# Packing the weight folds of a decoder kernel into earlier projection steps, and moving one memory head's transposes

## The chip, the cores and the metric

The kernel runs on one core of a Trainium2 chip. The metric is the device time of one execution in microseconds (us). A core has several engines that work at the same time, each through its own list of instructions in order: TensorE (PE in the rows of the profile: matmuls and transposes), VectorE (DVE), ScalarE (ACT: copies with scaling, and functions such as Exp, whose tables it must load first), GpSimd (POOL), and SyncE (SP), which issues nearly all DMAs of this kernel. An engine that reaches an instruction whose input is not there waits, and everything behind that instruction on the same engine waits with it.

## The reference, cut to what matters

One layer of a decoder for 2048 prompt tokens (and 32 sample tokens, which play no part here): a mixer, an attention to 256 memory tokens, and a gated MLP.

```
def mixer(xn, s0, lp):
    q, k, v, r, a, u, sv = split_cols(xn @ w_in)
    logg = jax.nn.log_sigmoid((a @ w_alpha + b_alpha)) / GLA_TAU
    o, S = gla_chunked(q, k, v, logg, s0)
    o = rmsnorm(o, g_gla_out).reshape(B, T, GLA_WIDTH) * jax.nn.silu(r)
    sv = rmsnorm(jax.nn.gelu(sv), g_sgu)
    s_out = jax.nn.gelu(u) * sgu_spatial(sv, w_s, b_s)
    return jnp.concatenate([o, s_out], -1) @ w_out, S, sv

def mem_kv(mem, g_mem, wk_x, wv_x):
    mn = rmsnorm(mem, g_mem)
    return mn @ wk_x, mn @ wv_x          # 256 x 4 heads x 256 each

def mem_attend(hn, mk, mv, wq_x, wo_x):
    q = hn @ wq_x
    p = softmax(q @ mk.T * MEM_DH ** -0.5)        # by head
    return (p @ mv) @ wo_x
```

## The kernel before, in words

**Numbers in two parts.** Each product of fp32 matrices is made of three matmuls on parts of lower precision (`mm3`, lines 100 to 102): high by high, high by low, low by high. So each weight that arrives is split: ACT copies it into a high part (`h_...`, line 85), DVE subtracts to get the low part (`l_...`, line 86). A weight tile of 128 x 1024 costs one such instruction on each of the two engines.

**Folding.** The scores of the memory attention are x wq mkT. The kernel multiplies wq by the memory keys once (`fold_qk`), and the memory values by wo once (`fold_vo`), writes both results to DRAM, and later streams them in as if they were weights. The keys and values of the four heads are made first (`mem_proj`, tiles mkp and mvp), turned by transposes for the output (mkt, mvt), and stored in DRAM (kd, vd) from which a fold loads them again (kr, vr; line 606). A fold of wq with keys is a pair of steps, for 4 heads x 2 halves: `turn_wq` loads a raw piece of wq (r_wqf) and transposes it (tile wqp; ACT and DVE split it into wqh and wql), and `fold_qk` makes 24 matmuls on two tiles qkp, which ACT copies (qkf) and splits (qkh). That gives 16 steps, `qk_steps`. A fold of wo with values is one step, again for 4 heads x 2 halves (`vo_steps`, 8 steps): a weight r_wof is split, 12 matmuls fill two tiles vop, which are split into voh and vol and put to DRAM.

**The order.** The prompt is worked on in four sub-blocks of 512 tokens. In the first one, the main steps are numbered 0 to 18: 0 to 3 the projection sv (four weights r_ws, tiles t_ws), 4 the projection a (tile ap), 5 k (weights r_wk, tiles a_wk), 6 q (r_wq, a_wq), 7 to 10 v (r_wv, t_wv), 11 and 12 u (a_wu), 13 to 16 r (t_wr), 17 and 18 the first half of the output projection (a_wo). A function `weave` puts side steps between them: `(steps, first, last)` spreads the steps evenly over main steps first to last. The side steps beside the folds are those of the gated linear attention: the gates of the decay (lgp on PE, then lgt on ACT: Abs, Exp, Ln for two halves, each Exp and each Ln behind a table load), the decayed keys and scores (e, kr, s, P), the state (ktp, kt, kv) and the outputs (op, o, otp), and the spatial gate (zp, z). Weights are loaded up to five units ahead of their step (`AHEAD`), into five raw buffers (`NRAW`) that come free when a weight is split. Within this written order a scheduler, at build time, sets the order of each engine's list; on the chip each engine follows its list strictly. The transposes `mkt` of a memory head stand in the steps of `mem_proj`, ahead of the first sub-block, where PE also turns the tokens themselves (xt, line 803).

The change touches `mem_proj` (line 577) and the line that sets the two spreads of the folds (line 1813). PSUM banks matter at two places: accumulators (`acc`: t_ws, a_wk, t_wv and so on) and the rest (`mps`: wqp, qkp, vop, lgp) have four banks each.

Of the kernel before, what the change touches and what calls it, by code (L numbers as in the profile page):

```python
# [38 lines left out]
def hymba_step_kernel(  # L39
# [22 lines left out]
    def U(name, dt=F32):  # L62
        return up.tile([128, TM], dt, tag="U", name=name)
# [7 lines left out]
    def acc(name):  # L71
        return accp.tile([128, 512], F32, tag="acc", name=name)

    def mps(name):
        return mmp.tile([128, 512], F32, tag="mm", name=name)
# [8 lines left out]
    def split(hi, lo, src, lo_eng=None):  # L84
        act.activation(hi, src, AF.Copy)  # L85
        (lo_eng or dve).tensor_tensor(lo, src, hi.bitcast(F32), ALU.subtract)  # L86
# [12 lines left out]
    def mm3(ps, wh, wl, xh, xl, first, last):  # L99
        out = pe.matmul(ps, wh, xh, start=first, stop=False)  # L100
        pe.matmul(ps, wh, xl, start=False, stop=False)  # L101
        pe.matmul(ps, wl, xh, start=False, stop=last)  # L102
        return out
# [23 lines left out]
    def wready(src, name):  # L127

        def load():
            out = []  # L130
            for x, tag in enumerate(("whi", "wlo")):
                t = wp.tile(list(src.shape[0:1]) + list(src.shape[2:]), F32R, tag=tag, name=f"{tag}_{name}")
                nc.sync.dma_start(t.bitcast(F32), src[:, x])
                out.append(t)
            return tuple(out)
        return load
# [220 lines left out]
    def keep(t, pattern, base, cm):  # L357
        pool.affine_select(out=t, in_=t, pattern=pattern, compare_op=ALU.is_ge, fill=0.0,
                           base=base, channel_multiplier=cm)
# [125 lines left out]
    def weave(main, *sides):  # L485

        out = []
        due = [0.0] * len(sides)
        at = [0] * len(sides)
        for i, m in enumerate(main):  # L490
            out.append(m)
            for j, (steps, first, last) in enumerate(sides):
                if i < first:
                    continue
                due[j] = len(steps) * min(1.0, (i - first + 1) / (last - first + 1))
                while at[j] < len(steps) and at[j] < due[j] - 1e-9:
                    out.append(steps[at[j]])
                    at[j] += 1
        for j, (steps, _, _) in enumerate(sides):
            out += steps[at[j]:]  # L500
        return out
# [33 lines left out]
    mem_st = NS_()  # L535
# [41 lines left out]
    def mem_proj(nm, h, od, *ws):  # L577

        th, tl, tf = U(f"m{nm}h{h}", F32R), U(f"m{nm}l{h}", F32R), U(f"m{nm}f{h}")
        for dt in range(2):  # L580
            ps = acc(f"m{nm}p{h}{dt}")
            ds_ = slice(dt * 128, (dt + 1) * 128)
            for k in range(8):
                wh, wl = ws[k // 4]
                mm3(ps[:, :256], wh[:, k % 4, ds_], wl[:, k % 4, ds_], *mem_st.pair[k], k == 0, k == 7)
            s = slice(dt * 256, (dt + 1) * 256)
            dve.tensor_tensor(tf[:, s], ps[:, :256], mem_st.bc[:, :256], ALU.mult)
            split(th[:, s], tl[:, s], tf[:, s])
        for x, t in enumerate((th, tl)):
            nc.sync.dma_start(kvd[nm, h][:, x], t[:, :512].bitcast(F32))  # L590
        if h % 2 == 0:
            mem_st.out[nm] = [U(f"m{nm}o{h}{c}") for c in range(2)]
        for c in range(2):
            ps = mps(f"m{nm}t{h}{c}")
            for d in range(2):
                pe.transpose(ps[:, d * 128:(d + 1) * 128], tf[:, d * 256 + c * 128:d * 256 + (c + 1) * 128], ident)
            dve.tensor_copy(mem_st.out[nm][c][:, (h % 2) * 256:(h % 2 + 1) * 256], ps[:, :256])
            if h % 2:
                nc.sync.dma_start(od[c * 128:(c + 1) * 128, (h - 1) * 256:(h + 1) * 256], mem_st.out[nm][c][:, :512])
# [60 lines left out]
    def fold_vo(h, jh, wu):  # L660

        if jh == 0:
            again("v", h)
        vh, vl = mem_st.t["v"]
        wh, wl = wu
        flush()
        for mt in range(2):
            ps = mps(f"vop{h}{jh}{mt}")
            for dt in range(2):
                a = dt * 256 + mt * 128  # L670
                mm3(ps, vh[:, a:a + 128], vl[:, a:a + 128], wh[:, dt], wl[:, dt], dt == 0, dt == 1)
            hi, lo = U(f"voh{h}{jh}{mt}", F32R), U(f"vol{h}{jh}{mt}", F32R)
            split(hi[:, :512], lo[:, :512], ps)
            kk = 2 * h + mt
            for x, t in enumerate((hi, lo)):
                put(vod[kk // 4][:, 2 * jh:2 * jh + 2, x, kk % 4],
                    t[:, :512].bitcast(F32).rearrange("p (m c) -> p m c", m=2))

    mem_steps = []
    for nm, w, od in (("k", wk_x, o_mem_k), ("v", wv_x, o_mem_v)):  # L680
        od = od[0, 0].rearrange("m h d -> m (h d)")
# [3 lines left out]
    qk_steps = []  # L685
    for h, j in ((2 * i + hh, j) for i in range(2) for j in range(2) for hh in range(2)):
        qk_steps.append(Step(lambda a, h=h, j=j: turn_wq(h, j, a), [wraw_unit(wq_x[0], 4 * j, 4, h * 256, 256, f"wqf{h}{j}")]))
        qk_steps.append(Step(lambda h=h, j=j: fold_qk(h, j)))
    vo_steps = [Step(lambda a, h=h, jh=jh: fold_vo(h, jh, a), [(wo_x[0], 2 * h, 2, jh * 512, 512, f"wof{h}{jh}")])
                for h in range(4) for jh in range(2)]  # L690
# [158 lines left out]
    def carry_sample(B, prev):  # L849

        def fn():
            for k in range(8):
                pool.tensor_tensor(B.h[k][:, SB:TM], prev.h[k][:, SB:TM], smp.d[:, k * NS:(k + 1) * NS], ALU.add)
        return Step(fn)
# [946 lines left out]
    for s, B in enumerate(blocks):  # L1801
        proj = proj_steps(B)
        gla, gtail = gla_steps(B)
        nlast = 4 if B.mix_sample else 3
        sgu_st = sgu_steps(B)
        nst = len(sgu_st) - 4
        keep = None
        if B.mix_sample:
            def keep():
                if not hasattr(smp, "x"):  # L1810
                    smp.x = U("smpx")
                return smp.x
        w1, w2, stat = out_proj_steps(B, lambda k0, m2, s=s: (w_out[0], k0, 4, m2 * 256, 256, f"wo{s}{k0}{m2}"),
                                      lambda B=B: B.cat, "gx", "wo", B.mix_sample, 4, B.mix_sample, keep, seven=True, whole=not B.mix_sample)
        early = [Step(sample_conv)] if B.ffn_sample else []
        folds = [(qk_steps, 0, 10), (vo_steps, 11, 19)] if s == 0 else []
        steps += weave(proj + w1, *folds, (after, 0, 5), (sgu_st[:1], 6, 6), (early, 1, 1), (sgu_st[1:nst], 11, 11), (sgu_st[nst:nst + 2], 12, 13), (sgu_st[nst + 2:], 16, 16), (gla[:1], 4, 4), (gla[1:2], 6, 6), (gla[2:12], 8, 10), (gla[12:-nlast], 10, 13), (gla[-nlast:], 16, 16), (gtail, 16 + B.mix_sample, 18 + B.mix_sample))
        scales, sc, turns = attention_steps(B)
        x1, x2, xstat = out_proj_steps(B, lambda k0, m2, s=s: wready(vod[k0 // 4][:, m2], f"wx{s}{k0}{m2}"),
                                       lambda B=B: B.ao, "gffn", "wx", False, 0, B.ffn_sample, seven=s > 0, whole=True)  # L1820
        steps += w2 + [stat, scales]
        steps += weave(sc + x1, (turns[:2], 8, 9), (turns[2:3], 13, 13), (turns[3:], 14, 14))
        fstart, fmain, flast = ffn_steps(B, s == NSB - 1)
        B.xstat = xstat.fn
        steps += x2 + ([xstat, fstart] if s == 0 else [])
        sides = []
        if B.mix_sample:
            sides.append((sample_steps(), 1, len(fmain) - 5))
        if s + 1 == NSB:
            ncs = conv_out_steps(carry, 2, o_state_conv[0, 0], "nc")  # L1830
            sides.append((ncs[:4], 30, 36))
        steps += weave(fmain[:-4], *sides)
        if s + 1 < NSB:
            after = final_steps(B)
            nxt = blocks[s + 1]
            norm = norm_in_steps(nxt)
            if nxt.ffn_sample:
                norm.append(carry_sample(nxt, B))
            steps += weave(fmain[-4:] + flast, (norm, 0, 4))
            if B.ffn_sample:  # L1840
                after += conv_out_steps(sct, 16, o_state_conv_s[0].rearrange("b t f -> (b t) f"), "ncs")
        else:
            steps += fmain[-4:-2] + flast[:1] + fmain[-2:] + ncs[4:] + flast[1:]
            after = []
# [30 lines left out]
```

## Time and profile before

| quantity | value |
|---|---|
| median of 3 runs | 2819.22 us (2818.85 to 2822.41) |
| the profiled execution's own time | 2823.05 us |
| its span (first to last instruction) | 2821.3 us |
| PE busy | 2784.2 us, 99% |
| DVE busy | 1902.5 us, 67% |
| ACT busy | 1108.3 us, 39% |
| POOL busy | 564.6 us, 20% |
| mean granted TensorE clock | 0.995 |

The stages that the change touches lie in the first 300 us: the memory heads and the tokens up to some 72 us, sv until 104, k and q until 140, v, u and r from there to 249, the output projection's first half from 271. Everything after that is the same program in both versions, except for what it inherits.

In rows of the trace the first number is the start in us from the beginning of the span, the second how long the instruction (or a run of like ones) took, then engine, line, operation, output and inputs with shapes; in square brackets the time that the engine had been idle before it, and what ended the wait.

### The profile page before, as it was taken

Reading aid. Unit: us, or ns where it says so; the run is one execution under the profiler, and the core shown is the slowest. Engines: PE = TensorE matmul, PEld = TensorE weight load, DVE = VectorE, ACT = ScalarE, POOL = GpSimd, SP = SyncE. Lnnn points to the kernel's source line nnn. Section 1 sums busy time; section 2 is a strip of 40 time slices with the busy share of each in tenths; the row PEclk is TensorE's granted clock in tenths of the full one; section 3 lists DMA queues with packets and bytes.
Section 4 is the critical chain, followed back from the end, with each engine's and each line's share of the span. In section 5 each row is a group of like instructions: output and inputs, shape, how many; then the busy total and the mean of one; then the engine's idle time right before and its main releaser. Section 6 shows DMA issues by size and latency. Waiting matters only on the chain.

```text
span 2821.3 us, 46765 instructions
## 1 busy us (share of the span) xinstructions
PE 2784.2 (99%) x17756; PEld 2459.7 (87%) x17756; DVE 1902.5 (67%) x3285; ACT 1108.3 (39%) x1948; POOL 564.6 (20%) x636
## 2 busy tenths in 40 slices
PE   8999999999999999999999999999999999999998
PEld 8787888888877898998888889899999788899997
DVE  6677778777657786655545778666666688665555
ACT  5645545333353444322223445422223645431222
POOL 1002212111101231322311121232221013132222
PEclk9999999999999999999999999999999999999999
DMA  9755589999942246888886325567776323577775
GB/s 296 245 193 195 174 262 332 341 340 348 351 129 62 83 145 214 305 292 291 318 315 214 93 66 193 209 243 258 255 266 227 109 75 137 202 261 274 271 281 181
DMA packets 369546, 638.06 MB, mean 226 GB/s; under 512 B 27356, under 2 KB 238272, under 8 KB 369322
## 3 DMA queue, kind: packets, MB, share of 16 engines
q1 hardware_dynamic: 369322, 635.07, 66.0%
q8 instruction: 141, 2.31, 0.3%
q14 instruction: 83, 0.68, 0.1%
HBM read 507.56 MB, written 127.41 MB: 225 GB/s over the span
## 4 chain that ended last, share of the span: by engine, by line
PE 90%; DVE 4%; DMA 2%; ACT 2%; issue 1%; POOL 1%; DVEq 0%; SPq 0%; ACTq 0%; POOLq 0%
PE d L102 6%; PE d L101 6%; PE d L100 6%; PE a_wx L101 2%; PE a_wx L100 2%; PE a_wx L102 2%; PE s L1063 2%; PE a_wup L101 1%; PE a_wg L101 1%; PE a_wup L102 1%; PE a_wg L102 1%; PE a_wg L100 1%; PE a_wup L100 1%; PE a_wu L100 1%; PE a_wu L102 1%
## 5 line engine op out<-in xcount | busy, mean ns | idle before, releaser
L100 PE MATMUL d<-acth,whi_wd 128*128 128x272 f32 (+1 forms) x688 | 235.5, 342 | 0.7 <-DVE h L1723 0.7
L1723 DVE TENSOR_TENSOR h<-d,h 128x512 f32<-128x512 f32 (+1 forms) x232 | 133.5, 582 | 150.2 <-PE d L102 150.0
L101 PE MATMUL d<-actl,whi_wd 128*128 128x272 f32 (+1 forms) x688 | 233.7, 340 | 0.0
L102 PE MATMUL d<-acth,wlo_wd 128*128 128x272 f32 (+1 forms) x688 | 233.5, 340 | 0.0
L1616 POOL TENSOR_TENSOR c<-c,bc_f 128x512 f32<-128x512 f32 (+1 forms) x88 | 136.1, 1550 | 141.9 <-ACT c L1615 141.2
L1606 ACT ACTIVATE c<-g,colsb 128x512 f32<-128x512 f32 x88 | 71.7, 815 | 190.0 <-DVE g L1569 142.9
L102 PEld LDWEIGHTS d<-acth,wlo_wd 128*128 128x128 f32 x688 | 129.2, 188 | 15.5 <-issue 1.2
L100 PEld LDWEIGHTS d<-acth,whi_wd 128*128 128x128 f32 x688 | 129.4, 188 | 15.3 <-DVE h L1723 1.2
L101 PEld LDWEIGHTS d<-actl,whi_wd 128*128 128x128 f32 x688 | 129.4, 188 | 13.8 <-issue 0.4
L1638 POOL TENSOR_TENSOR c<-r_q_wup,c 128x512 f32<-128x512 f32 (+1 forms) x33 | 62.4, 1891 | 328.9 <-DVE r_q_wup L297 209.2
L1603 POOL COPY carry<-g 128x2 f32<-128x2 f32 x88 | 32.2, 366 | 420.3 <-DVE g L1569 416.3
L100 PE MATMUL a_wo<-ch,h_wo 128*128 128x512 f32 (+1 forms) x320 | 111.3, 361 | 1.8 <-ACT ch L89 1.4
L101 PE MATMUL a_wo<-cl,h_wo 128*128 128x512 f32 (+1 forms) x320 | 112.0, 353 | 0.0
L102 PE MATMUL a_wo<-ch,l_wo 128*128 128x512 f32 (+1 forms) x320 | 111.4, 351 | 0.0
L1607 DVE SCALAR_TENSOR_TENSOR c<-g,colsb,c 128x512 f32<-128x512 f32 x88 | 85.8, 975 | 28.4 <-ACT c L1606 27.8
L85 ACT ACTIVATE acth<-c 128x512 fp32r<-128x512 f32 (+1 forms) x88 | 55.6, 636 | 117.6 <-DVE c L1638 82.8
L102 PE MATMUL a_wx<-pTh,wlo_wx 128*128 128x512 f32 x256 | 101.1, 395 | 0.0
L101 PE MATMUL a_wx<-pTl,whi_wx 128*128 128x512 f32 x256 | 100.6, 393 | 0.0
L100 PE MATMUL a_wx<-pTh,whi_wx 128*128 128x512 f32 x256 | 100.2, 394 | 0.0
L1608 DVE SCALAR_TENSOR_TENSOR c<-g,colsb,c 128x512 f32<-128x512 f32 x88 | 92.9, 1055 | 1.1
L1615 ACT ACTIVATE c<-c 128x512 f32<-128x512 f32 (+1 forms) x88 | 56.1, 638 | 91.7 <-DVE c L1608 79.7
L86 DVE TENSOR_TENSOR actl<-c,acth 128x512 fp32r<-128x512 f32 (+1 forms) x88 | 64.0, 732 | 25.5 <-ACT acth L85 24.2
(3754 smaller groups left out, 9702.9 us busy)
## 6 DMA issues: line engine op xcount, KB each, us to landing
whi_wd<-wd SPq DMA_DIRECT2D x66, 512.0 KB
wlo_wd<-wd SPq DMA_DIRECT2D x66, 512.0 KB
r_wo<-in_w_out_dram SPq DMA_DIRECT2D x32, 512.0 KB
wlo_wx<-vod SPq DMA_DIRECT2D x32, 512.0 KB
whi_wx<-vod SPq DMA_DIRECT2D x32, 512.0 KB
r_wg<-in_w_gate_dram SPq DMA_DIRECT2D x22, 512.0 KB
r_wup<-in_w_up_dram SPq DMA_DIRECT2D x22, 512.0 KB
r_wd<-in_w_down_dram SPq DMA_DIRECT2D x22, 512.0 KB
```

Of the source, the lines that this page charges most:

```text
L86: (lo_eng or dve).tensor_tensor(lo, src, hi.bitcast(F32), ALU.subtract)
L100: out = pe.matmul(ps, wh, xh, start=first, stop=False)
L101: pe.matmul(ps, wh, xl, start=False, stop=False)
L102: pe.matmul(ps, wl, xh, start=False, stop=last)
L1063: pe.matmul(ps3[:, :, c * 64:(c + 1) * 64], kl[:, c * 128:(c + 1) * 128], kr3[:, :, c * 64:(c + 1) * 64], start=True, stop=True)
L1606: act.activation(c[:, :SB], g[:, 2:SB + 2], AF.Identity, bias=cb, scale=w2)
L1607: dve.scalar_tensor_tensor(c[:, :SB], g[:, 1:SB + 1], w1, c[:, :SB], ALU.mult, ALU.add)
L1608: dve.scalar_tensor_tensor(c[:, :SB], g[:, 0:SB], w0, c[:, :SB], ALU.mult, ALU.add)
L1615: act.activation(c[:, :T], c[:, :T], AF.Gelu_apprx_tanh)
L1616: pool.tensor_tensor(c[:, :T], c[:, :T], B.fbc[:, :T], ALU.mult)
L1638: (dve, pool)[i].tensor_tensor(c[:, :T], q[i], c[:, :T], ALU.mult)
L1723: dve.tensor_tensor(B.h[m + mm][:, cs], ps[:, :cw], B.h[m + mm][:, cs], ALU.add)
```

## The change

Two edits. The transposes and copies of a memory head move from `mem_proj` into a function of their own, `mem_turn`. For the first key head nothing is turned in its own step; it is turned in the step of the second key head, just ahead of that one's. And in the first sub-block the 16 steps of the wq folds are spread over main steps 0 to 6 in place of 0 to 10, the 8 steps of the wo folds over 6 to 12 in place of 11 to 19.

```
@@ mem_proj @@
         for x, t in enumerate((th, tl)):
             nc.sync.dma_start(kvd[nm, h][:, x], t[:, :512].bitcast(F32))
+        if (nm, h) == ("k", 0):
+            mem_st.wait = tf
+            return
+        if (nm, h) == ("k", 1):
+            mem_turn("k", 0, od, mem_st.wait)
+        mem_turn(nm, h, od, tf)
+
+    def mem_turn(nm, h, od, tf):
+
         if h % 2 == 0:
             mem_st.out[nm] = [U(f"m{nm}o{h}{c}") for c in range(2)]
         for c in range(2):
@@ the steps of a sub-block @@
-        folds = [(qk_steps, 0, 10), (vo_steps, 11, 19)] if s == 0 else []
+        folds = [(qk_steps, 0, 6), (vo_steps, 6, 12)] if s == 0 else []
```

The number of instructions of each kind on each engine stays what it was. What the scheduler made of the new order differs on PE, DVE and ACT up to the end of the attention's first pass (about 300 us) and is identical from there on. Lines behind the edit have numbers higher by 9. Three places show how the lists moved.

**The gates.** PE's list right after the two products lgp that feed the gates, before:

```order
L102 MATMUL qkp_1601<-kr_1554,wql_1573 128x256
L986 MATMUL lgp_1628<-aT_1533,wal 128x512
L986 MATMUL lgp_1634<-aT_1533,wal 128x512
L100 MATMUL a_wk_1685<-xh_6_1166,h_wk_1347 128x512
L101 MATMUL a_wk_1685<-xl_6_1167,h_wk_1347 128x512
L102 MATMUL a_wk_1685<-xh_6_1166,l_wk_1348 128x512
L100 MATMUL a_wk_1685<-xh_7_1170,h_wk_1347 128x512
L101 MATMUL a_wk_1685<-xl_7_1171,h_wk_1347 128x512
L102 MATMUL a_wk_1685<-xh_7_1170,l_wk_1348 128x512
L100 MATMUL a_wq_1748<-xh_0_1063,h_wq_1459 128x512
```

and in the changed kernel (wqp are transposes of a piece of wq for the next fold, wqh its high part, which ACT makes, qkp the fold's products):

```order
L995 MATMUL lgp_1776<-aT_1681,wal 128x512
L995 MATMUL lgp_1782<-aT_1681,wal 128x512
L100 MATMUL a_wq_1965<-xh_7_1166,h_wq_1698 128x512
L101 MATMUL a_wq_1965<-xl_7_1167,h_wq_1698 128x512
L102 MATMUL a_wq_1965<-xh_7_1166,l_wq_1699 128x512
L626 MATMUL wqp_1870<-ident,r_wqf_1523 128x128 x4
L626 MATMUL wqp_1879<-ident,r_wqf_1523 128x128 x4
L100 MATMUL qkp_1888<-kr_1866,wqh_1875 128x256
L101 MATMUL qkp_1888<-kr_1868,wqh_1875 128x256
```

Before, the rest of k and all of q (a_wk, a_wq: 54 matmuls) stood between the gates' products and the next fold's products; now three matmuls and eight transposes do. On ACT the list at this place holds the same rows in both versions up to the two wqh: four gate functions' table loads and activations, and wqh behind the third of them.

**The end of sv.** PE's list behind the last product of t_ws, before (ap is the projection a, which needs only the tokens):

```order
L102 MATMUL t_ws_1214<-h_ws_1223,xl_7_1171 128x512
L100 MATMUL qkp_1495<-kr_1427,wqh_1436 128x256
L101 MATMUL qkp_1495<-kr_1429,wqh_1436 128x256
L100 MATMUL qkp_1514<-kr_1427,wqh_1436 128x256
L101 MATMUL qkp_1514<-kr_1429,wqh_1436 128x256
L102 MATMUL qkp_1495<-kr_1427,wql_1437 128x256
L102 MATMUL qkp_1514<-kr_1427,wql_1437 128x256
L891 MATMUL ap_1534<-h_0_428,wa 32x512
```

In the changed kernel a whole fold stands there (qkp_1453 and qkp_1472, 24 rows), then at once the next one (qkp_1557, qkp_1582), whose wqh_1506 ACT makes in this order, from the copy of the first fold's products on (r_wq is a raw weight that must have landed):

```order
L649 ACTIVATE qkf_1466<-qkp_1453 128x512
L85 ACTIVATE qkh_1467<-qkf_1466 128x512
L649 ACTIVATE qkf_1485<-qkp_1472 128x512
L85 ACTIVATE h_wq_1609<-r_wq_1607 128x1024
L85 ACTIVATE qkh_1486<-qkf_1485 128x512
L85 ACTIVATE wqh_1506<-wqp_1501 128x512
L85 ACTIVATE wqh_1515<-wqp_1510 128x512
L903 ACT_TABLE_LOAD
L903 ACTIVATE sv_1531<-t_ws_1193,xrs_417 128x512
```

The projection a moved behind the k projection, 120 rows on.

**The loads ahead of sv.** SP's list of DMAs, before (r_ws_1221 is the fourth and last weight of sv; out and kd, vd are the memory heads' outputs and stores, kr the keys that a fold loads again):

```order
L111 DMA r_ws_1073<-in_w_in_dram 128x2x512
L111 DMA r_wqf_1191<-in_wq_x_dram 128x4x256
L599 DMA out_dram<-mko_625 128x512
L599 DMA out_dram<-mko_626 128x512
L606 DMA kr_1227<-kd_159 128x512
L606 DMA kr_1229<-kd_159 128x512
L111 DMA r_ws_1221<-in_w_in_dram 128x2x512
L590 DMA vd_164<-mvh_906 128x512
L111 DMA r_wqf_1287<-in_wq_x_dram 128x4x256
```

and in the changed kernel (r_ws_1283 is the fourth weight of sv):

```order
L111 DMA r_wqf_1073<-in_wq_x_dram 128x4x256
L111 DMA r_ws_1187<-in_w_in_dram 128x2x512
L608 DMA out_dram<-mko_625 128x512
L608 DMA out_dram<-mko_626 128x512
L615 DMA kr_1223<-kd_159 128x512
L615 DMA kr_1225<-kd_159 128x512
L111 DMA r_wqf_1221<-in_wq_x_dram 128x4x256
L590 DMA vd_164<-mvh_906 128x512
L111 DMA r_ws_1283<-in_w_in_dram 128x2x512
```

One piece of wq went ahead of the last weight of sv, which now stands two rows further back.

The wo folds' products (vop, 96 matmuls) moved with their loads. Before, 12 stood beside u, 24 beside r and 60 behind the state's second transposes (ktp): 36 right behind these, 24 among the outputs op and the first products of a_wo. In the changed kernel 60 stand beside v, 24 beside u, 12 at the start of r, and none behind the second ktp.

The first key head's transposes (mkt) still stand on PE right behind the two products mbc that spread the memory's norm (both ahead of the second head's products); four transposes of tokens (xt) that stood behind them now stand ahead of them.

## The prediction

> **What bounds the kernel now.** I read the page first: the busy time of each engine, then the chain that ended last.
>
> ```profile
> PE 2784.2 (99%) x17756; PEld 2459.7 (87%) x17756; DVE 1902.5 (67%) x3285; ACT 1108.3 (39%) x1948; POOL 564.6 (20%) x636
> ...
> PE 90%; DVE 4%; DMA 2%; ACT 2%; issue 1%; POOL 1%; DVEq 0%; SPq 0%; ACTq 0%; POOLq 0%
> ```
>
> PE is busy 2784.2 of 2821.3 us, so 37.1 us of idle is all that reordering could win, beside the time that matmuls spend at a lower clock. The change adds and removes no matmul: its worth is the PE idle that it ends, less the PE idle that it makes. Next come the windows (columns: length, busy time of PE, PEld, DVE, ACT, POOL, granted clock, DMA share, GB/s) and the list of PE's waits, both for the first 330 us, since everything behind is the same list of instructions.
>
> ```profile
> 20.00:40.00 20.00, 17.22 (x135) 17.06 (x134) 13.12 (x27) 10.43 (x22) 3.60 (x11) 0.91 0.98 314
> ...
> 100.00:120.00 20.00, 18.27 (x110) 14.36 (x109) 9.63 (x18) 16.10 (x49) 0.00 (x0) 1.00 0.87 280
> 120.00:140.00 20.00, 20.00 (x101) 16.25 (x100) 16.25 (x35) 16.31 (x23) 2.90 (x1) 1.00 0.74 232
> ...
> 180.00:200.00 20.00, 20.00 (x115) 17.23 (x113) 17.10 (x34) 6.64 (x12) 2.72 (x2) 1.00 0.54 165
> ...
> 240.00:260.00 20.00, 14.07 (x68) 11.84 (x67) 16.12 (x26) 6.32 (x11) 4.80 (x3) 0.76 0.40 131
> 260.00:280.00 20.00, 20.00 (x102) 16.42 (x101) 12.25 (x19) 11.47 (x17) 5.25 (x4) 0.89 0.81 276
> 280.00:300.00 20.00, 16.43 (x86) 13.46 (x85) 16.39 (x29) 10.02 (x15) 4.91 (x4) 0.96 0.69 217
> ```
>
> ```profile
> PE s L1063 <- DVE kr L1053: 5.0, 2, 3.3
> ...
> PE mkt L596 <- DVE mkf L587: 2.8, 1, 2.8
> PE otp L1210 <- DVE vol L86: 2.4, 1, 2.4
> PE a_wk L100 <- ACT sv L894: 1.3, 1, 1.3
> ...
> PE ktp L1102 <- POOL kh L1099: 0.9, 1, 0.9
> PE otp L1210 <- DVE o L1204: 0.7, 1, 0.7
> ...
> PE a_wo L100 <- ACT ch L89: 0.5, 1, 0.5
> PE qkp L102 <- DVE wql L86: 0.4, 1, 0.4
> ```
>
> The reader is to see two things. Between 120 and 240 us PE idles nowhere (two of the six windows are shown): folds, projections and the decay's chain cover one another there. And the idle near the edited part is in three places: at the first head's transposes (2.8), at the end of sv (0.4 + 1.3), and from 248 to 300, where PE waits for the decay, the state and the outputs (5.0 + 0.9 + 2.4 + 0.7 + 0.5 = 9.5) and the granted clock falls to 0.76.
>
> **The change, part by part.** *The gates.* This is the largest term. Their rows before, PE's first, then ACT's:
>
> ```profile
> 125.06 1.88 PE L986 MATMUL lgp<-aT,wal 128*128 128x512 f32 x4
> 126.37 0.80 PE L100 MATMUL a_wk<-xh,h_wk 128*128 128x512 f32 x1
> ...
> 131.15 0.60 PE L617 MATMUL wqp<-ident,r_wqf 128*128 128x128 f32 x4
> 131.50 0.48 PE L102 MATMUL a_wq<-xh,l_wq 128*128 128x512 f32 x1
> 131.81 0.39 PE L100 MATMUL a_wq<-xh,h_wq 128*128 128x512 f32 x1
> 132.05 0.39 PE L101 MATMUL a_wq<-xl,h_wq 128*128 128x512 f32 x1
> ...
> 140.11 0.28 PE L100 MATMUL qkp<-kr,wqh 128*128 128x256 f32 x1
> ```
>
> ```profile
> 126.12 0.69 ACT L987 ACTIVATE lgt<-lgp,colsb 128x512 f32<-128x512 f32 x1 [1.00 <-PE lgp L986]
> ...
> 127.31 1.28 ACT L992 ACT_TABLE_LOAD   x1
> 128.60 0.63 ACT L992 ACTIVATE lgt<-lgt 128x512 f32<-128x512 f32 x1
> ...
> 134.86 0.58 ACT L85 ACTIVATE wqh<-wqp 128x512 fp32r<-128x512 f32 x1
> ```
>
> ACT cannot begin the gates before lgp, and the next fold's wqh stands behind three of the four table loads: it is done at 134.86 + 0.58 = 135.44, which is 10.4 us after lgp began. Before, PE had a_wk and a_wq to do until 140.11, so this cost nothing. In the changed order PE has, from lgp's start, 1.31 (126.37 - 125.06) for lgp, 0.24 for each of three a_wq (132.05 - 131.81), and 0.42 for each of two groups of wqp (0.35 to the next start, and 0.07 that the row behind takes longer), in all 2.9. ACT's rows ahead of wqh are the same ones. So qkp, and all of t_wv behind it, waits 10.4 - 2.9 = **+7.5**. Bounds: 5.9 if the weight split and the copy that stand among the gates (1.06 and 0.58 in the rows further down) fall out of the way (7.5 - 1.6), 7.6 if PE's groups run at their shortest.
>
> The Trainium skill, "ScalarE: Activation LUTs", section "What ACT_TABLE_LOAD costs", counts 1283 ns for a load and 1380 ns more for a drain at each switch. The rows disagree on the drain: the load of 127.31 ends at 128.59 and the function starts at 128.60. With that drain this wait would be 4.1 longer, by the page's figures, an estimate; the rows decide.
>
> *The end of sv.* Here the fold's own chain is what counts:
>
> ```profile
> 100.50 0.28 PE L102 MATMUL qkp<-kr,wql 128*128 128x256 f32 x1
> 100.62 0.28 PE L100 MATMUL qkp<-kr,wqh 128*128 128x256 f32 x1
> ...
> 107.84 1.28 ACT L894 ACT_TABLE_LOAD   x1
> 109.13 2.42 ACT L894 ACTIVATE sv<-t_ws,xrs 128x512 f32<-128x512 f32 x4
> ```
>
> ```profile
> 92.01 1.06 ACT L85 ACTIVATE h_wq<-r_wq 128x1024 fp32r<-128x1024 f32 x1 [4.59 <-DMA r_wq<-in_w_in_dram]
> 92.98 0.58 ACT L640 ACTIVATE qkf<-qkp 128x512 f32<-128x512 f32 x1
> 93.59 0.63 ACT L85 ACTIVATE qkh<-qkf 128x512 fp32r<-128x512 f32 x1
> ...
> 99.33 1.06 ACT L85 ACTIVATE h_wq<-r_wq 128x1024 fp32r<-128x1024 f32 x1 [2.99 <-DMA r_wq<-in_w_in_dram]
> ```
>
> From the last product of qkp_1453 to wqh_1506 ACT does qkf, qkh, qkf, h_wq, qkh, wqh: 0.58 + 0.63 + 0.58 + 1.06 + 0.63 + 0.58 = 4.1. PE has 7 products of 0.12 (100.62 - 100.50) and one group wqp, 1.3: a wait of 2.8. Then a_wk needs a bank that sv frees behind wqh, a table load and the first sv (0.58 + 1.28 + 0.6 = 2.5), against 1.6 of products: 0.8, in place of the 1.3 of before; and the 0.4 of before goes. Third, h_wk and h_wq stand ahead of the wqh on ACT and wait for their DMAs; before ACT lost 4.59 and 2.99 at such places without harm to PE, now PE stands behind them. I take 2.9, the shorter of the two rows, from 0 to 4.6. Sum 2.8 + 0.8 - 1.7 + 2.9 = **+4.8**, from 1.9 to 6.5.
>
> *The start of sv.*
>
> ```profile
> 64.39 0.38 SPq L111 DMA_DIRECT2D r_ws<-in_w_in_dram  x1
> ...
> 67.08 0.38 SPq L111 DMA_DIRECT2D r_wqf<-in_wq_x_dram  x1
> ```
>
> ```profile
> 70.36 1.06 ACT L85 ACTIVATE h_ws<-r_ws 128x1024 fp32r<-128x1024 f32 x1 [1.85 <-PE mvp L101]
> ```
>
> The fourth weight of sv takes the place of the piece of wq that was issued 2.7 later. Its split stands on ACT ahead of the parts xh of the tokens, without which sv cannot start. So sv starts later by the 2.7, less what ACT has waited for anyway: **+1.5**, from 0 to 2.7.
>
> *The fold behind the gates.* The same chain as at sv, without a weight: from the last product of qkp_1888, qkf, qkh, qkf, qkh, wqh = 3.0 on ACT against 7 products and one group on PE, 1.3: **+1.7**, from 0 to 3.
>
> *The first head's transposes.* They still stand behind mbc; what moved is four transposes of tokens (under 0.9), from behind the wait to inside it: **-0.5**, from -0.9 to 0.
>
> *The stage 240 to 300.* The scores wait for kr on DVE, and one row leaves their way:
>
> ```profile
> 252.22 1.21 DVE L86 TENSOR_TENSOR l_wof<-r_wof,h_wof 128x1024 fp32r<-128x1024 f32 x1
> ```
>
> That takes 1.2 from the wait for the second kr, and the last outputs no longer wait for a vol (2.4 in the list), of which I count 0.4, since the products that filled PE ahead of it go too. But the 60 products vop that PE did here, 60 x 0.24 = 14.4 us of work, are gone too: they filled the time from ktp to kv, and now PE has only zp and the first a_wo. Net **-1.6**, from -6 (all waits of 9.5 but 3.5 gone) to +2 (a new wait for kt and z where vop stood).
>
> *The clock.* Where PE idled the windows show 0.91, 0.76, 0.89, 0.96; a wait of 2.8 alone (the only one from 20 to 40) went with 0.91, which is 20 x 0.09 / 0.5 = 3.6 us at half speed. Work at half speed takes twice its time, so such a stretch costs 1.8. I count one for the gates' wait and a small share for those at sv: **+2.0**, from 0 (waits too short) to 5 (three).
>
> The Trainium skill, "TensorE: Matmul & The Clock Gate", section "What's actually happening", lets the clock fall after a whole idle window of about 3.4 us. By that only the gates' wait would cool PE, and the term would be 1.8; the row of 0.91 shows a fall with 2.8, so the trace doesn't bear the bound out.
>
> Sum: 7.5 + 4.8 + 1.5 + 1.7 - 0.5 - 1.6 + 2.0 = +15.4 against the profiled execution's 2823.05: 2838.4. That execution lies 3.8 above the median 2819.2; on the median's scale it is 2819.2 + 15.4 = **2834.6**.
>
> PE work that could hide the waits is what the change moved away; DVE (16.25 of 20 at 120 to 140) and DMA (0.74 there) take on the wo folds' splits and loads in this stage. I cost these at nothing because DVE has 2.9 of 20 free even in its fullest window shown, 180 to 200; without that cover, a weight split of 1.21 on the way is the price of each.
>
> **The rivals.** *Only the gates.* Loads land in time, and ACT, ahead by the gates' wait, has later pieces ready: 7.5 + 1.8 for the clock - 1.6 is +7.7, **2826.9**. For it: PE's idle at one place lets every other engine catch up. Against it: the chain at sv needs no load to cost 2.8.
>
> *The tail pays.* If DVE, freed of the wo folds, ends the kr in time, the 9.5 us of waits from 248 to 300 fall to 3.5, below what lowered the clock, and half of the clock's price goes as well: 0.24 + 0.11 + 0.04 of 20 us is 7.8, half 3.9. That is -10 in place of -1.6: 15.4 + 1.6 - 10 = +7 with all other terms, -1 with the gates alone (7.5 + 1.8 - 10); between them +3, **2822**, no change that can be told. Against it: scores, ktp and zp stand back to back with nothing between.
>
> *The other side: PE's waits are DVE's gain.* In the stage 240 to 300 PE waits for DVE, and DVE works on while PE stands at the gates. If from there on DVE is never held by PE, it is 7.5 ahead when PE comes to the last scores, all 9.5 of waits and the whole 7.8 of the clock go, and if the same lead covers loads (2.9), sv's start (1.5) and the new clock term (2.0), the sum is 15.4 + 1.6 - 9.5 - 7.8 - 2.9 - 1.5 - 2.0 = -6.7: **2812.5**, faster. It decides from the point where kr stands ready when s comes up. Against it: kr needs e and b, whose gates hang on the same lgp, and DVE gets the wo folds' splits in just this stretch.
>
> *A backlog.* DMAs of wo beside those of v (0.74 to 0.87 share now) delay r_wv: two waits of the 4.6 seen above: +9 on the sum, **2843.6**.
>
> *The first head's turn* may not be later at all: the order shows it where it was. This is inside my -0.5.
>
> **How the numbers follow.** What a measurement of this kernel can tell from no change is about 0.2%, 5.6 us. Forecast 2834.6 (from 2829 to 2841): 0.52. Only the gates, 2826.9: 0.20. Tail pays, 2822: 0.13. Faster, 2812.5: 0.07. Backlog, 2843.6: 0.08. The terms' lower ends add up to about 0 and their upper ends to +27; the range **2818 to 2845** takes in these but the faster one and the outer part of the backlog. Slower by over 0.2% (above 2824.9): 0.52 + 0.08 + 0.18 of the second case = 0.78. Same: 0.02 + 0.12 = 0.14. Faster: 0.07 + 0.01 = 0.08.
>
> **What would show it right or wrong.** In the profile after: a wait of qkp for ACT wqh of some 7 us behind lgp (near 135 to 145); waits of qkp for wqh of 2 to 3 near 105, with a_wk's for sv below 1; sv's last weight split 1 to 3 later than the 70.36 of before; at the second ktp no vop, and PE's waits there of 5 to 8 in all. Wrong: no wait at the gates, because ACT or the order there differs from my reading; or waits from 248 to 300 under 5 with the clock at 1.00, which makes the tail's rival true.

## The result, and the profile after

The changed kernel takes 2848.56 us (median of 5 runs, 2842.61 to 2850.09), the kernel before beside it 2819.63 (2818.85 to 2822.41): a ratio of 1.0091, with a 95% interval from 1.0079 to 1.0103. It is slower, by 26 us by the ratio and 29 by the medians. The forecast was slower too, 2834.6, but its range ended at 2845.

The busy times of the profiled execution (its own time 2842.61, the shortest of the five), as in the first rows of before:

```profile
span 2840.9 us, 46753 instructions
PE 2789.0 (98%) x17756; PEld 2463.9 (87%) x17756; DVE 1895.3 (67%) x3285; ACT 1108.5 (39%) x1948; POOL 571.5 (20%) x636
```

PE's idle is 2840.9 - 2789.0 = 51.9 us, 14.8 more than before; its busy time grew by 4.8 for the same matmuls, so some of them ran longer. The windows of the first 300 us (same columns as before) say where:

```profile
60.00:80.00 20.00, 16.34 (x108) 14.18 (x107) 16.15 (x33) 11.34 (x22) 0.00 (x0) 1.00 0.88 311
...
100.00:120.00 20.00, 13.39 (x64) 11.64 (x63) 9.21 (x18) 9.96 (x16) 0.00 (x0) 0.79 0.82 251
120.00:140.00 20.00, 20.00 (x107) 15.79 (x106) 11.83 (x21) 13.63 (x44) 3.01 (x1) 0.96 0.83 271
140.00:160.00 20.00, 16.68 (x96) 13.85 (x94) 8.04 (x17) 11.05 (x17) 0.00 (x0) 0.98 0.78 239
160.00:180.00 20.00, 14.52 (x67) 12.16 (x68) 11.19 (x23) 10.57 (x15) 1.30 (x1) 0.76 0.42 126
```

The rows of before for the last two of these windows (the prediction has those from 100 and from 120):

```profile
140.00:160.00 20.00, 20.00 (x120) 17.61 (x119) 16.67 (x30) 11.22 (x21) 1.33 (x1) 1.00 0.80 256
160.00:180.00 20.00, 20.00 (x124) 17.69 (x124) 14.70 (x28) 9.17 (x21) 0.00 (x0) 1.00 0.65 218
```

Between 100 and 180, where PE had idled 1.7 us before, it idles 15.4, and the granted clock, 1.00 there before, falls to 0.79 and 0.76. No other engine is full in these windows: DVE is busy 8.0 to 11.8 of 20 us, ACT 10.0 to 13.6, and the DMA share is 0.42 to 0.83 (before 0.65 to 0.87). So the order is the first suspect. PE's waits from 60 to 330:

```profile
PE qkp L100 <- ACT wqh L85: 13.2, 4, 7.0
PE s L1072 <- DVE kr L1062: 4.2, 2, 3.5
PE otp L1219 <- DVE o L1213: 3.9, 1, 3.9
PE qkp L102 <- DVE wql L86: 2.1, 2, 1.4
PE t_ws L100 <- ACT xh L89: 2.0, 1, 2.0
...
```

Folds that wait for the high part of their transposed wq, 13.2 us in four waits, are the new item. The longest is the one behind the gates, in PE's rows, with ACT's wqh that it waits for behind them:

```profile
153.24 1.88 PE L995 MATMUL lgp<-aT,wal 128*128 128x512 f32 x4
154.55 0.80 PE L100 MATMUL a_wq<-xh,h_wq 128*128 128x512 f32 x1
...
155.65 1.03 PE L626 MATMUL wqp<-ident,r_wqf 128*128 128x128 f32 x8
163.66 0.58 PE L100 MATMUL qkp<-kr,wqh 128*128 128x256 f32 x1 [6.98 <-ACT wqh L85]
...
164.68 0.63 PE L100 MATMUL t_wv<-h_wv,xh 128*128 128x512 f32 x1
...
169.37 0.43 PE L101 MATMUL t_wv<-l_wv,xh 128*128 128x512 f32 x1
169.64 0.40 PE L102 MATMUL t_wv<-h_wv,xl 128*128 128x512 f32 x1
```

```profile
163.03 0.58 ACT L85 ACTIVATE wqh<-wqp 128x512 fp32r<-128x512 f32 x1
```

qkp starts 163.66 - 153.24 = 10.4 us behind lgp, as the gates' chain on ACT had it before. And the reader sees the second price: from 163.66 to 169.4 each matmul with 512 columns takes 0.63 in place of 0.39 us and starts 0.43 behind the one ahead of it, in place of 0.23. So a wait of 7 us is followed by 5.7 us of work at about half speed. Windows cut to the stretches in which the granted clock is at half show the same, and two more such stretches at the end of sv:

```profile
108.00:114.80 6.80, 6.16 (x28) 5.94 (x28) 2.21 (x4) 1.86 (x4) 0.00 (x0) 0.50 0.67 196
118.25:121.60 3.35, 3.35 (x13) 3.16 (x14) 0.52 (x1) 2.97 (x7) 0.00 (x0) 0.50 0.98 301
159.25:169.40 10.15, 5.74 (x16) 4.68 (x17) 8.29 (x18) 6.71 (x8) 0.00 (x0) 0.50 0.59 177
```

The waits at the end of sv begin with one of 2.70 at 106.52. ACT's rows show that a load stands behind it: the wqh comes behind a weight of k that ACT had to wait for.

```profile
104.00 1.06 ACT L85 ACTIVATE h_wk<-r_wk 128x1024 fp32r<-128x1024 f32 x1 [4.41 <-DMA r_wk<-in_w_in_dram]
...
105.89 1.07 ACT L85 ACTIVATE wqh<-wqp 128x512 fp32r<-128x512 f32 x2
```

### The profile page after: what moved, and what is told of

Read it like the earlier page. It is cut to its first block, busy times and chain, and to the rows that moved or that the text cites. A ratio compares the mean times of both kernels' runs of the same rounds, so it can differ in the third digit from the quotient of the medians.

```text
span 2840.9 us, 46753 instructions
## 1 busy us (share of the span) xinstructions
PE 2789.0 (98%) x17756; PEld 2463.9 (87%) x17756; DVE 1895.3 (67%) x3285; ACT 1108.5 (39%) x1948; POOL 571.5 (20%) x636
## 4 chain that ended last, share of the span: by engine, by line
PE 91%; DVE 4%; ACT 2%; DMA 2%; issue 1%; POOL 1%; DVEq 0%; SPq 0%; ACTq 0%; POOLq 0%
PE d L101 6%; PE d L100 6%; PE d L102 6%; PE a_wx L101 2%; PE a_wx L102 2%; PE a_wx L100 2%; PE s L1072 2%; PE a_wg L100 1%; PE a_wup L100 1%; PE a_wg L101 1%; PE a_wg L102 1%; PE a_wup L101 1%; PE a_wup L102 1%; PE a_wo L100 1%; PE a_wo L101 1%; PE a_wo L102 1%
## 5 line engine op out<-in xcount | busy, mean ns | idle before, releaser
L1625 POOL TENSOR_TENSOR c<-c,bc_f 128x512 f32<-128x512 f32 (+1 forms) x88 | 142.3, 1623 | 134.6 <-ACT c L1624 133.9
L102 PEld LDWEIGHTS d<-acth,wlo_wd 128*128 128x128 f32 x688 | 129.6, 188 | 15.5 <-issue 1.2
L100 PEld LDWEIGHTS d<-acth,whi_wd 128*128 128x128 f32 x688 | 129.4, 188 | 15.4 <-DVE h L1732 1.2
L1616 DVE SCALAR_TENSOR_TENSOR c<-g,colsb,c 128x512 f32<-128x512 f32 x88 | 86.7, 985 | 27.8 <-ACT c L1615 27.2
L1617 DVE SCALAR_TENSOR_TENSOR c<-g,colsb,c 128x512 f32<-128x512 f32 x88 | 86.1, 978 | 1.1
```

The lines of the kernel that those rows point to most:

```text
L1616: dve.scalar_tensor_tensor(c[:, :SB], g[:, 1:SB + 1], w1, c[:, :SB], ALU.mult, ALU.add)
L1617: dve.scalar_tensor_tensor(c[:, :SB], g[:, 0:SB], w0, c[:, :SB], ALU.mult, ALU.add)
L1625: pool.tensor_tensor(c[:, :T], c[:, :T], B.fbc[:, :T], ALU.mult)
```

## The experiments

Medians are compared with runs of the kernel before on the same chip: 2821.3 for e1 to e4, 2821.9 for e5 to e10.

### The changed kernel once more, and each part alone

No edit in the first. The second and the third take one spread each:

```
e2:  folds = [(qk_steps, 0, 6), (vo_steps, 11, 19)]      # turn as before
e3:  folds = [(qk_steps, 0, 10), (vo_steps, 6, 12)]      # turn as before
e5:  folds = [(qk_steps, 0, 10), (vo_steps, 11, 19)]     # mem_turn as in the change
```

> The changed kernel once more, whole. Its profiled execution took 2842.6 us and three of its five runs 2848.6 to 2850.1. If the spread is that of the lowered clock (theory: PE's new waits each lower the granted clock, more or less often by where they fall in the clock's windows of 3.41 us), this profile shows the same waits of PE within 1 us each (7.0 behind the gates, 6.6 in all at the end of sv, 1.7 at the next fold) and another time at half speed. If the spread is that of the loads (rival), the waits themselves differ by 3 us or more in sum.

> Only the wq folds moved (0 to 6); wo folds and the first head's transposes as before. My theory: nearly all of the loss is here, since the waits of qkp for wqh behind the gates and at the end of sv come from the wq folds' order: 2819.6 + 26 to 31, so 2845 to 2851, with a wait near 7 us behind lgp. Rival (the wo folds' loads and splits, put beside v, are what costs): 2819.6 + 8 to 15.

> Only the wo folds moved (6 to 12). My theory: the tail's gain alone, -1.7 us as measured from the end of r to the second ktp, and no wait at the gates: 2815 to 2821. Rival (wo folds cost): 2830 to 2838, with new waits of PE between 140 and 240 us.

> Only the first key head's transposes moved; both spreads of folds as before. My theory: in the order they still stand behind mbc, so nothing changes that a measurement can tell: 2818 to 2823 beside 2821.3, with a wait of mkt for mkf between 1.1 and 2.8 us as in the other profiles. Rival (the later turn holds up the start of sv): sv starts 2 us or more later and the median is above 2824.

| kernel | median us | ratio to before (95%) |
|---|---|---|
| e1, the change again | 2849.46 | 1.0100 (1.0086 to 1.0113) |
| e2, wq folds alone | 2845.55 | 1.0086 (1.0072 to 1.0099) |
| e3, wo folds alone | 2821.11 | 0.9995 (0.9986 to 1.0005) |
| e5, first head's turn alone | 2822.75 | 1.0000 (0.9991 to 1.0009) |

The wq folds alone make 24 of the 28 us of the loss; the wo folds alone and the turn alone do nothing that can be told. The last 4 us (e1's four runs all lie above e2's, though two of the first five of the changed kernel do not) stand in no part alone; pairs of parts were not tried. The turn's kernel still waits for mkf at its transposes, 2.0 us, within the 1.1 to 2.8 of the other profiles. Its sv starts at 71.73, in the profile before at 72.35, but in five kernels without the turn that wait there no more than 0.2 for xh (e3, e6, e8 to e10) at 69.3 to 70.5; so 1 to 2 us at this place are not ruled out, though the median shows none.

The second profile of the changed kernel (2848.19 us) is 5.6 us longer than the first. PE's busy time and its waits from 60 us on:

```profile
PE 2793.9 (98%) x17756; PEld 2467.2 (87%) x17756; DVE 1897.5 (67%) x3285; ACT 1109.2 (39%) x1948; POOL 571.0 (20%) x636
```

```profile
PE qkp L100 <- ACT wqh L85: 13.5, 4, 7.0
PE s L1072 <- DVE kr L1062: 4.2, 2, 3.5
PE otp L1219 <- DVE o L1213: 3.9, 1, 3.9
PE t_ws L100 <- ACT xh L89: 3.0, 1, 3.0
...
PE qkp L102 <- DVE wql L86: 1.1, 2, 0.9
```

The waits differ by 1 us at two places, in opposite directions (t_ws, the start of sv, 3.0 and 2.0; qkp for wql, 1.1 and 2.1), and by less at the others; PE's busy time differs by 4.9. So it is mostly the matmuls' own time that spreads, as expected of the clock: in this run the matmuls behind the wait of 3.03 at 73 took 0.63 too, in the first, behind one of 1.96, they did not. The rival, loads that land at other times, has the 1 us at sv's start.

### The gates moved behind the k and q projections

```
-(gla[:1], 4, 4)
+(gla[:1], 6 if s == 0 else 4, 6 if s == 0 else 4)
```

> The changed kernel, with the gates of the first sub-block put behind main step 6 in place of 4, so that their table loads no longer stand ahead of the folds' wqh on ACT. My theory: the wait of 7.0 us behind lgp goes, and with it the half speed that follows (about 2): 9 us less than the changed kernel, 2836 to 2841. Rival (ACT is late for its loads in any case, so another wait takes its place at the same fold): 0 to 3 less, with a wait of qkp for wqh of 4 us or more near 155. A second rival: the decay starts later by 25 us and is late at the scores in v: new waits of s for kr near 190 to 210.

2844.82 us, ratio 1.0085 (1.0072 to 1.0099): 4.6 less than the change again, and outside my 2836 to 2841. The 7.0 is gone, but the fold at that place still waits 1.7, and three new waits stand in this kernel's list from 60 to 260:

```profile
PE qkp L100 <- ACT wqh L85: 7.3, 4, 2.9
PE s L1072 <- DVE kr L1062: 4.4, 2, 3.1
...
PE t_wv L100 <- DVE k L889: 1.7, 1, 1.7
PE a_wu L100 <- DVE v L888: 1.2, 1, 1.2
```

The scores s wait for kr in the middle of v (4.4) now that the decay starts later, and half speed comes with that wait. The second rival was right beside the theory: the wait was the gates', and taking them out of the way makes the decay late. PE's idle is the same as in the change again, 2842.5 - 2790.0 = 52.5 against 52.6: waits of the same length took the place of the 7.0, and what was gained is the matmuls' own time (2790.0 against 2793.9).

### A middle dose

```
folds = [(qk_steps, 0, 8), (vo_steps, 11, 19)]
```

> Only the wq folds, spread over main steps 0 to 8 in place of 10 (the changed kernel: 6). In this order 45 matmuls of k and q stand behind the gates' products before the next fold's, and its wqh's transposes stand ahead of them; behind sv one whole fold stands with its weights already split, then k. My theory (what counts is what stands between an input's making and its use): no wait at the gates, 2 to 4 us at the end of sv: 2823 to 2829. Rival (the density of the folds itself costs, by DMA and ACT): about half the way to the 2845.6 of the wq folds alone, 2831 to 2836.

2831.07 us, ratio 1.0031 (1.0019 to 1.0042), 9.2 above before: just what the rival (density) said, and outside my 2823 to 2829. The places are mine, though, and the sizes are not. There is no wait behind the gates, as the order had it; all of it is at the end of sv:

```profile
PE a_wk L100 <- ACT sv L894: 2.7, 1, 2.7
PE qkp L100 <- ACT wqh L85: 2.1, 1, 2.1
PE qkp L102 <- DVE wql L86: 1.9, 1, 1.9
```

```profile
100.00:120.00 20.00, 13.28 (x55) 11.25 (x54) 9.92 (x18) 13.54 (x24) 0.00 (x0) 0.74 0.87 282
```

The waits sum to 6.7 (before: 1.7), and half speed in this one window takes 0.26 x 20 = 5 us of matmul time, part of it while PE idled anyway. As at the end of sv in the changed kernel, the wait for wqh goes back to a DMA: ACT's rows show the load of q's weight, which stands ahead of the wqh, holding ACT up for 6.27 us. So the rival has more than its number here: a late load is part of the wait, and this run does not part it from the cover.

```profile
100.85 1.06 ACT L85 ACTIVATE h_wq<-r_wq 128x1024 fp32r<-128x1024 f32 x1 [6.27 <-DMA r_wq<-in_w_in_dram]
...
103.68 1.07 ACT L85 ACTIVATE wqh<-wqp 128x512 fp32r<-128x512 f32 x2
```

### Each piece of wq turned one fold ahead

The steps of the wq folds alternate turn, fold, turn, fold. Here they run turn 0, turn 1, fold 0, turn 2, fold 1 and so on, so that the transposes, the splits and the load of the keys are written a fold earlier than the products that need them; the spreads stay those of the change (e7) or of before (e8).

```
 in turn_wq:   again("k", h)
+              mem_st.t["k", h, j] = mem_st.t["k"]
 in fold_qk:
-    kh, kl = mem_st.t["k"]
+    kh, kl = mem_st.t.pop(("k", h, j))
 the steps:
+    qk_steps = turns[:1]
+    for x, y in zip(turns[1:], qkf):
+        qk_steps += [x, y]
+    qk_steps += qkf[-1:]
```

> The changed kernel with each piece of wq transposed and split one fold ahead of its use (its keys are loaded a fold earlier too). My theory: the waits of qkp for wqh come from transposes, split and products standing back to back; behind the gates a_wk and a_wq stand again, so that wait of 7.0 and the 1.7 of the next fold go, with some 3 of half speed: 2834 to 2840 in place of 2849. At the end of sv the scheduler still puts the products right behind the transposes, so 2 to 4 us stay there. Rival (ACT and DVE are late as such): the waits of 13 us for wqh move elsewhere and the median stays above 2845.

> The kernel before with the same turning one fold ahead. PE waits there for wqh or wql only 0.4 us, and the chain of the tail is untouched: 2817 to 2823, no change that can be told. If it is below 2816, half speed between 100 and 120 or the wait of a_wk for sv was worth more than the waits show.

e7: 2818.97 us, ratio 0.9990 (0.9981 to 0.9999). It is level with before and 30 us below the change again, where I expected 9 to 15. Its busy time and its waits from 60 to 330:

```profile
PE 2781.7 (99%) x17756; PEld 2458.1 (87%) x17756; DVE 1899.2 (67%) x3285; ACT 1107.1 (39%) x1948; POOL 571.2 (20%) x636
```

```profile
PE otp L1224 <- DVE o L1218: 2.7, 2, 2.4
PE t_ws L100 <- ACT xh L89: 2.5, 1, 2.5
PE otp L1224 <- DVE o L1166: 2.3, 1, 2.3
PE ktp L1116 <- POOL kh L1113: 1.0, 1, 1.0
...
PE vop L102 <- DMA vr<-vd: 0.7, 1, 0.7
```

No fold waits for wqh or wql any more, neither behind the gates nor at the end of sv, and PE's busy time is 12.2 us below that of e1 for the same matmuls: the lowered clock went with the waits. Of the change's waits those at the start of sv (2.5) and of the outputs otp (2.7 + 2.3, in the change 3.9) stay; the last scores' wait for kr (4.2 in the change) went too, and why is not shown. The DMA share from 100 to 180 is higher in this kernel than in the changed one (1.05 and 0.90, against 0.82 and 0.83, in the windows from 100 and from 120), and ACT still stands 3.69 us for a weight of k with a wqh right behind it:

```profile
103.20 1.06 ACT L85 ACTIVATE h_wk<-r_wk 128x1024 fp32r<-128x1024 f32 x1 [3.69 <-DMA r_wk<-in_w_in_dram]
104.17 1.07 ACT L85 ACTIVATE wqh<-wqp 128x512 fp32r<-128x512 f32 x2
```

PE does not wait for it. So late loads or density alone are not the cause: they cost in the changed order, where the products stand right behind the wqh. What this run does not separate is which of the three things written earlier (transposes, splits, keys) matters most, since the build's scheduler moved other rows as well.

e8: 2808.67 us, ratio 0.9950 (0.9937 to 0.9964), the fastest kernel here. My expectation of no change was wrong, and so was the reason that I kept open for a gain at half speed between 100 and 120: the granted clock there is 1.00 before, too. PE's waits from 60 to 330:

```profile
PE otp L1215 <- DVE vol L86: 2.5, 1, 2.5
PE ktp L1107 <- POOL kh L1104: 1.8, 1, 1.8
...
PE otp L1215 <- DVE o L1209: 0.5, 1, 0.5
PE s L1068 <- ACT h_wof L85: 0.3, 1, 0.3
```

The 0.4 and 1.3 at the end of sv went, and so did the 5.0 that the last scores waited for kr; the granted clock from 240 to 260 and from 260 to 280, 0.76 and 0.89 before, is 1.00 in both. In this kernel's order 34 matmuls of r stand between the spatial gate's products and these scores, where before 13 did; that is 21 x 0.24 = 5 us more of work for PE while DVE makes kr. That the longer cover is why the wait went is read from the order and the trace; it was not tried apart.

e7 and e8 differ by the change alone, and e7 is 10.3 us slower (idle 36.3 against 28.7, PE busy 2781.7 against 2778.8). So the turning ahead takes the change's cost from 28 us to 10, and does not end it; e7 is level with before only because turning ahead wins 13 us in the order of before, too.

### The tail once more

```
e9:   e8 with (vo_steps, 11, 16)
e10:  e8 with (vo_steps, 11, 17)
```

> The kernel before with the turning one fold ahead (2808.7 us) and the wo folds spread over 11 to 16 in place of 11 to 19: no product of them is left among the outputs, 48 stand behind the second ktp. My theory (a wait goes where its input is made earlier): the wait of otp for vol, 2.45 us, goes, and half speed behind it: 2803 to 2808. Rival (the wait moves to the outputs o themselves, as in the changed kernel, where otp waited 3.9 us for o): 2808 to 2813.

> The same with the wo folds over 11 to 17: 36 products stand behind ktp, 12 among the outputs, none right ahead of otp. My theory: 2804 to 2809, the wait of otp for vol smaller than 2.45. Rival (otp waits for o in its place): 2808 to 2813.

2812.50 (ratio 0.9968, 0.9956 to 0.9980) and 2810.25 (0.9963, 0.9951 to 0.9976): both no better than e8, as the rivals said. The wait of otp for vol goes, and otp waits for the outputs o in its place, here in e9:

```profile
PE otp L1215 <- DVE o L1209: 2.9, 2, 2.0
PE ktp L1107 <- POOL kh L1104: 1.4, 1, 1.4
PE otp L1215 <- DVE o L1157: 1.3, 1, 1.3
```

## Why the prediction was right in its places and wrong in its size

The direction and the mechanism held: the wq folds, drawn together, stand right behind what makes their inputs. By the steps of the sum, against the two profiles of the changed kernel:

- **The gates, +7.5**: 6.98 in both. Right, and so was reading the load of a table as 1.28 with no drain behind it.
- **The end of sv, +4.8**: the waits there are 2.70 + 1.38 + 1.80 + 0.72 = 6.6 in the first profile and 6.0 in the second, against 1.7 before: +4.9 and +4.3. The term for loads, 2.9, was right in kind and size: the 2.70 stands behind k's weight. The rest of the sum came right by luck. The second fold waited 1.80 in the first profile (2.38 in the second) in place of 2.8, since ACT copied the first of the two tiles qkp while PE still made the second; a_wk's wait for sv, 0.8 in my sum, did not come at all; and the waits for wql, 1.38 + 0.72 (0.90 + 0.24), which my sum did not have, made up for both.
- **The fold behind the gates, +1.7**: 1.71 in both. Right.
- **The stage 240 to 300, -1.6**: from the last row of r to the second ktp 10.0 us before and 8.3 after, -1.7; nothing more behind it (the waits of the outputs are 3.9, before 2.4 + 0.7 + 0.5). The kernel with this part alone is level with before, so the rival "the tail pays" fell.
- **The first head's transposes, -0.5**: the wait for mkf is 1.1 to 2.3 in every later profile, with the turn and without, and the 2.8 of the profile before was the longest. The turn does nothing that the median shows.
- **The start of sv, +1.5 (0 to 2.7)**: t_ws waits 1.96 and 3.03 for xh, and 2.5 to 3.1 in e7 and e2, where before it waited for nothing but the 0.2 for xl. The mechanism was right: sv's last split h_ws waits for its load, 3.08 in the first profile. The size was too small; 2.7 less the 1.85 that ACT had waited before is 0.85, so my 1.5 was a guess between that and 2.7. Where half speed follows the wait it costs more still.
- **The clock, +2.0 (0 to 5)**: this is the step that failed, by size. I counted one stretch of 3.6 us at half speed behind the gates and "a small share" for sv's end. In the first profile PE worked 5.74 us at half speed behind the gates, and 6.16 + 3.35 in two stretches at the end of sv; at half speed these 15.2 us cost 7.6 more than at full, an estimate. PE's busy time over the whole span, for the same matmuls, grew by 4.8 in the first profile and 9.7 in the second. The sum in the second is 15.5 of idle, where the terms without the clock gave 13.4, and 9.7 of slower matmuls, where I had 2.0: 25.2, which is 2848.2 - 2823.05.

So the idle was forecast within some 2 us, and the range missed because the term of the clock, 2.0 with an upper end of 5, came out at 9.7: only the wait at the gates had been given a full price. The first profile, with 4.8, lies inside the range. Between the forecast 2834.6 and the second profile's 2848.2 lie 7.7 us of clock, 2.1 of idle, and 3.8 that I had taken off to come from the profiled execution of before to the median of its three runs, 2819.2; later sets of runs have that median at 2821.3 to 2821.9. Some of the waits for wqh, wql and xh went with half speed and some did not; a term that can come out at 5 or at 10 from one run to the next should have had 10 as its upper end. That the busy time belongs to the waits, and not to the folds' place as such, e7 shows: with the same spreads and no wait for wqh or wql it is 2781.7, below that of before.

The rival "only the gates" fell with the waits at sv. "A backlog" has the number nearest to the result, 2843.6, but not the cause: PE waits for no weight of v, and the wo folds alone cost nothing (e3). The rival "PE's waits are DVE's gain" fell too: DVE had 9.2 of 20 us busy in the window from 100 and did not come early to the last scores (4.2 of waits for kr, 5.0 before).

The Trainium skill, "TensorE: Matmul & The Clock Gate", section "What's actually happening", lets the clock fall after an idle window of about 3.4 us. Here waits of 2.70 and 1.38 close together went with 0.79 from 100 to 120, and e6's 2.1, 1.9 and 2.7 with 0.74. The measurements differ from this statement, and decide: by the page the end of sv would have cost no clock at all.

## What to carry to other kernels

When an order is packed tighter, look at each place for what stands between the making of an input and its use on the engine that is the bound; that cover is what the denser order spent here, where no other engine was full. Writing a chain of turn, split and multiply one stage ahead paid in both orders here: the dense one went from 28 us above before to level with it, the loose one to 0.5% below it. And price a wait of TensorE at its length plus the slower matmuls behind it, with a range for whether the clock falls.

## What had not been expected of the hardware

The granted clock fell to half at waits of PE of 2 to 3 us, but not at each of them. In the changed kernel's first profile it fell at 108.0, in the wait of 1.38 that follows the one of 2.70; in the second at 108.8, inside a single wait of 2.46. At the start of sv waits of 1.96, 2.2 and 2.5 (the first profile, e4, e7) left it at 1.00 in the window from 60 to 80, and waits of 3.03 and 3.1 (the second profile, e2) went with 0.91 and 0.83. What decides is not shown here. The price was of the order of the waits themselves: in e6, 6.7 us of waits went with a granted clock of 0.74 in the window from 100. And two profiles of one kernel differ by 4.9 us in the matmuls' own time, 2789.0 and 2793.9, with each wait within some 1 us of its like.
